# Value products of two attentions as unsplit float32, two query tiles on the two column halves of the array

## The chip, the cores and the metric

One core of a Trainium2 chip runs the whole program in one launch. The metric is the device time in microseconds (us), the median of the runs shown. TensorE (PE) multiplies; VectorE (DVE), ScalarE (ACT) and GpSimd (POOL) do the rest; SyncE (SP) issues most of the loads. Each engine works through its own instructions in order and waits on semaphores for the others.

## The reference, cut to what matters

Two layers run over 512 latent tokens and 256 context tokens, 1024 wide. In each, one projection feeds three head groups, and their outputs are concatenated and projected back. The change touches the last product of two of these groups, probabilities times values:

```
# neighbourhood attention: 8 heads of 64; a query sees 8 x 16 grid neighbours and all 256 context keys
p = softmax(concat([s_loc, s_ctx]))
out = einsum(p[..., :n_keys], v_g) + einsum(p[..., n_keys:], vc)
# differential attention: 4 heads of 64 (two queries and keys of 32); keys are 512 latent + 256 context
p = softmax(s1) - lam * softmax(s2)
out = einsum('bhqk,bkhe->bqhe', p, v)
```

Context tokens attend to the 256 context tokens alone, with the same weights, and only in layer 0, since their result is not needed after it. Everything is float32.

## The kernel before, in words

A large float32 product is made of three passes over split operands: a helper `split` (line 70) writes the value rounded to the short format `F32R` with ACT (line 71, a cast) and the remainder with DVE or POOL (line 75, a subtraction); the three products high x low, high x high and low x high are then summed in PSUM. A product of plain float32 tiles is also possible; the profile shows it as two records of each instruction where an `F32R` product has one.

The stages of a layer, in order: norm and input projection, Fourier groups, differential attention (about 163 to 280 us in layer 0, 1218 to 1330 in layer 1), neighbourhood attention (280 to 452 and 1330 to 1470), output projection, feed-forward. The change lies in the two attention stages.

Both attentions work through steps (head, query tile of 128): tiles 0 to 3 are latent tokens; in layer 0 a fifth step per head handles the 256 context queries. Step n does, in program order:

- `scores` of a later step: the products q k into PSUM, the row maximum (DVE), the exponential (ACT), for differential attention also the mix of two exponentials (DVE, lines 822 to 825);
- `values` of step n-1: the product with the values into bank `do` or `o` (lines 889 and 1154), in a bank, 64 partitions x 512 columns, for the four latent tiles and a bank of its own for the context tile;
- `turn` of step n: PE transposes the probabilities (lines 868, 874 and 1133) into PSUM, and `split` evicts them as high and low part, `dph` or `ph`.

The values of a head are split once per head, by `prep_v` and `values_in`, with ACT and POOL (tiles `dvh`, `vh`). When the last tile of a head is done, ACT copies the bank to `yT` (lines 895, 897, 1093). A latent tile of differential attention has 6 key blocks of 128, so 18 products of 64 x 128; of neighbourhood attention 4 key blocks, so 12. The context tile has 2 key blocks, so 6 products of 64 x 256. The softmax of neighbourhood attention is divided after the values, by `divide` (line 978).

Between steps, `fill` hands PE units of the input projection of later heads (`projection`, line 649, tile `nacc`), so that it has work while DVE and ACT make probabilities. In the second half of neighbourhood attention these are used up, and chunks of the modulation (line 143, tile `m`) stand there, each a product with 32 stationary columns for four column groups of the array. The order on each engine is fixed when the program is built, by a list scheduler that follows dependencies and the priority of program order; pools of two or a few buffers decide what can run ahead.

Of the kernel before, what the change touches and what calls it, by code (L numbers as in the profile page):

```python
# [11 lines left out]
F32 = mybir.dt.float32  # L12
I32 = mybir.dt.int32
F32R = mybir.dt.float32r
# [15 lines left out]
NAH = 8  # L30
# [19 lines left out]
def hybrid_kernel(ctx: ExitStack, tc: tile.TileContext, A, out, dbg=None, stop=None):  # L50
# [409 lines left out]
    for l in range(DEPTH):  # L460
        first, last = l == 0, l == DEPTH - 1
        SL, SR = ("left", "right") if first else ("right", "left")
        nq = 4 if last else 6
# [247 lines left out]

        with ExitStack() as es:
# [62 lines left out]
        with ExitStack() as es:  # L775
            sk = pool(es, f"dstk{l}", 1)
            tq = pool(es, f"dtq{l}", 2)
            wk = pool(es, f"dwk{l}", 1)
            ek = pool(es, f"dek{l}", 2)
            dvp = pool(es, f"dvh{l}", 1)  # L780
# [30 lines left out]

            def prep_v(h):
                vh = dvp.tile([128, 6, 2, 64], F32R, tag="dvh", name="dvh")
                for t0, dv in ((0, dvx), (4, dvc)):
                    n = dv.shape[1]
                    split(vh[:, t0:t0 + n, 0], vh[:, t0:t0 + n, 1], dv[:, :, h * 64:(h + 1) * 64], lo="p")
                return vh
# [41 lines left out]

            def turn(i, e):  # L860
                nonlocal pace
                ph = [wk.tile([128, 768 if i < 4 else 512], F32R, tag=f"dph{z}", name="dph") for z in range(2)]
                ph4 = [p if i < 4 else p.rearrange("p (c i q) -> p c i q", c=2, i=2) for p in ph]
# [12 lines left out]
                return ph  # L876

            def values(h, i, ph):
                nonlocal pace, prev, o, vh
                y = od[h // 2][64 * (h % 2):64 * (h % 2) + 64]  # L880
                if i == 0:
                    vh = prep_v(h)
                    o = po.tile([128, 512], F32, tag="o", name="do")
                    prev = None
                oi, c0, n = (o[0:64, i * 128:i * 128 + 128], 0, 128) if i < 4 else \
                    (po.tile([128, 256], F32, tag="o", name="doc")[0:64], 4, 256)
                jobs = [(vz, pz_, c) for vz, pz_ in ((0, 1), (0, 0), (1, 0)) for c in range(6 - c0)]
                for k, (vz, pz_, c) in enumerate(jobs):
                    pace = pe.matmul(oi, lhsT=vh[:, c0 + c, vz], rhs=ph[pz_][:, c * n:(c + 1) * n],  # L889
                                     start=k == 0, stop=k == len(jobs) - 1)  # L890
                    if k == 0 and i < 4:
                        after(pace, prev)
                prev = pace
                if i == 3:
                    sc.copy(y[:, 0:512], o[0:64])
                elif i == 4:
                    sc.copy(y[:, 512:768], oi)

            pace = prev = o = vh = None
# [25 lines left out]
            values(*steps[-1], ph.pop(n))  # L925
# [72 lines left out]
        with ExitStack() as es:  # L998
# [7 lines left out]
            php = pool(es, f"php{l}", 2)  # L1006
# [42 lines left out]
            def prepare(h):  # L1049
# [5 lines left out]
                H[h] = qT, kT, bia, tq  # L1055
# [29 lines left out]
            def values_in(h):  # L1085
                hs = slice(h % 4 * 64, h % 4 * 64 + 64)
                vh = H[h][3].tile([128, 6, 2, 64], F32R, tag="vh", name="vh")
                split(vh[:, :, 0], vh[:, :, 1], vs[h // 4][:, :, hs], lo="p")
                return vh

            def emit_y(h, o, off, n):
                p0 = 64 * (h % 2)
                sc.copy(yT[h // 2][p0:p0 + 64, off:off + n], o[0:64, 0:n])

            def scores(h, i):
                nonlocal pace
                qT, kT, bia, _ = H[h]
# [31 lines left out]
            def turn(i, sb):  # L1129
# [9 lines left out]
            def values(h, i, ph):  # L1139
                nonlocal pace, prev, o, vh  # L1140
                if i == 0:
                    o = po.tile([128, 512], F32, tag="o", name="o")
                    prev = None
                if i < 4:
                    oi = o[0:64, i * 128:(i + 1) * 128]
                    ks = [(t, c, 1) for c, t in enumerate((i, i + 1, 4, 5) if i < 3 else (4, 5, 0, 3))]
                else:
                    oc = po.tile([128, 256], F32, tag="o", name="oc")
                    oi = oc[0:64].rearrange("p (j q) -> p j q", j=2)
                    ks = [(4, 0, 2), (5, 2, 2)]  # L1150
                n = 0
                for vz, pz_ in ((0, 1), (0, 0), (1, 0)):
                    for t, c, w in ks:
                        pace = pe.matmul(oi, lhsT=vh[:, t, vz], rhs=ph[pz_][:, c:c + w],  # L1154
                                         start=n == 0, stop=n == 3 * len(ks) - 1)
                        if n == 0 and i < 4:
                            after(pace, prev)
                        n += 1
                prev = pace
                if i == 3:  # L1160
                    emit_y(h, o, 0, 512)
                elif i == 4:
                    emit_y(h, oc, 512, 256)
                if i == ni - 1 and h + 1 < NAH:
                    vh = values_in(h + 1)
# [8 lines left out]
            vh = values_in(0)  # L1174
# [6 lines left out]
            for n, (h, i) in enumerate(steps):  # L1181
# [28 lines left out]
                if n:  # L1210
                    values(*steps[n - 1], ph.pop(n - 1))
# [18 lines left out]
            values(*steps[-1], ph.pop(n))  # L1230
# [346 lines left out]
```

## Time and profile before

| | before |
|---|---|
| runs, us | 1916.23, 1918.22, 1919.35 (median 1918.22) |
| profiled execution, us | 1918.2, of which the span from first to last instruction is 1916.4 |
| PE busy | 1807.5 us, 94% of the span |
| DVE, ACT, POOL busy | 1273.3, 788.9, 638.7 us |
| mean granted TensorE clock | 0.983 of full speed |

A row of the grouped view gives line, engine, operation, tile written and tiles read, stationary size and shape, count, then the busy time of the group (overlaps counted once), the mean duration of one, and the idle time of the engine just before, with what ended it. Products are pipelined: their durations overlap, so what one costs in a row of equal ones is the distance between starts, which a timeline shows.

### The profile page before, as it was taken

How to read it: one execution, taken by the hardware profiler on the slowest of the kernel's cores; microseconds unless marked ns; L12 is line 12 of the kernel's file. 1: busy time of each engine (PE TensorE's matmuls, PEld its weight loads, DVE VectorE, ACT ScalarE, POOL GpSimd, SP SyncE). 2: the span in 40 equal slices, each digit the busy share in tenths (PEclk: the TensorE clock that was granted, in tenths of full speed). 3: DMA queues.
4: the chain of work that ended last, by engine and by line, in shares of the span. 5: the costliest groups of instructions: out<-in, count | busy, mean ns of one | idle time of the engine just before them, and what ended most of it. 6: DMA issues, size and time to landing. Idle time of an engine off the chain costs nothing.

```text
span 1916.4 us, 28921 instructions
## 1 busy us (share of the span) xinstructions
PE 1807.5 (94%) x11297; PEld 1528.1 (80%) x11297; DVE 1273.3 (66%) x2494; ACT 788.9 (41%) x1470; POOL 638.7 (33%) x830
## 2 busy tenths in 40 slices
PE   6998989999999999999999989898998999999997
PEld 4787889867877888888888878788987778888885
DVE  4576865566466777767777694686556567777775
ACT  3326755565244222222222252585666243333331
POOL 3465636432141211211111164473833232121122
PEclk9999999999999999999999999999999999999999
DMA  9351021166016322432333013211243233232311
GB/s 284 111 174 45 24 39 32 33 228 194 24 42 204 117 95 97 159 101 73 105 110 110 29 44 112 71 45 36 57 131 122 90 110 110 88 110 88 96 37 44
DMA packets 146720, 183.11 MB, mean 96 GB/s; under 512 B 38200, under 2 KB 108672, under 8 KB 145560
## 3 DMA queue, kind: packets, MB, share of 16 engines
q1 hardware_dynamic: 107056, 157.83, 25.6%
q0 software_dynamic: 5888, 20.26, 3.5%
q10 hardware_dynamic: 33640, 3.19, 1.4%
q8 instruction: 89, 1.46, 0.3%
q14 instruction: 47, 0.39, 0.1%
HBM read 179.07 MB, written 8.07 MB: 98 GB/s over the span
## 4 chain that ended last, share of the span: by engine, by line
PE 79%; DVE 8%; DMA 4%; ACT 3%; issue 2%; POOL 2%; SPq 0%; ACTq 0%; DVEq 0%; POOLq 0%
PE u L1342 25%; PE dps L1406 14%; PE nacc L649 9%; PE uc L1342 6%; PE oacc L1280 6%; PE bank L533 3%; PE o L1154 2%; PE m L143 2%; PE s L1111 1%; DMA w<-w_in 1%; PE tpp L1133 1%; PE do L889 1%; DVE dmx L840 1%; PE u L731 1%; DVE e L825 1%
## 5 line engine op out<-in xcount | busy, mean ns | idle before, releaser
L1342 PE MATMUL u<-hx,uwh 128*128 128x512 f32 (+2 forms) x2160 | 518.5, 393 | 7.8 <-ACT hx L421 2.2
L1342 PEld LDWEIGHTS u<-hx,uwh 128*128 128x128 f32 x2160 | 401.4, 189 | 102.6 <-issue 3.4
L1410 POOL TENSOR_TENSOR res<-res,dm 128x512 f32<-128x512 f32 x110 | 155.8, 1417 | 594.5 <-DVE dm L1409 588.8
L1406 PE MATMUL dps<-wd,gt 128*128 128x512 f32 x1320 | 324.2, 395 | 6.8 <-DVE wd L75 2.8
L1406 PEld LDWEIGHTS dps<-wd,gt 128*128 128x128 f32 x1320 | 248.2, 190 | 64.4 <-DVE dm L1409 4.8
L649 PE MATMUL nacc<-wh,hx 128*128 128x256 f32 x1536 | 212.9, 288 | 4.7 <-ACT wh L71 2.7
L1371 DVE SCALAR_TENSOR_TENSOR ob<-u,cvc,ob 128x504 f32<-128x504 f32 x352 | 153.1, 477 | 93.7 <-ACT ob L1368 92.6
L649 PEld LDWEIGHTS nacc<-wh,hx 128*128 128x128 f32 x1536 | 194.6, 192 | 7.7 <-ACT wh L71 3.1
L1409 DVE TENSOR_TENSOR dm<-dps,g 128x512 f32<-128x512 f32 x220 | 147.9, 684 | 62.0 <-PE dps L1406 58.7
L1368 ACT ACTIVATE ob<-u,cvc 128x512 f32<-128x512 f32 x88 | 68.4, 778 | 200.2 <-PE u L1342 200.2
L1342 PEld LDWEIGHTS uc<-hc,uwh 128*128 128x128 f32 x1056 | 130.3, 190 | 7.5 <-issue 1.7
L1342 PE MATMUL uc<-hc,uwh 128*128 128x256 f32 x1056 | 133.5, 283 | 1.1 <-POOL hc L422 0.5
L75 POOL TENSOR_TENSOR wh<-w,wh 128x512 fp32r<-128x512 f32 x70 | 92.6, 1339 | 56.1 <-ACT wh L71 56.0
L71 ACT CAST uwh<-w 128x1024 fp32r<-128x1024 f32 x88 | 91.2, 1043 | 36.3 <-DMA w<-w_up 23.9
L1280 PE MATMUL oacc<-owh,yh 128*128 128x512 f32 x320 | 101.5, 403 | 1.2 <-DVE y L978 0.8
L75 DVE TENSOR_TENSOR uwh<-w,uwh 128x1024 fp32r<-128x1024 f32 x74 | 96.7, 1313 | 7.4 <-ACT uwh L71 5.8
L71 ACT CAST gt<-g 128x768 fp32r<-128x768 f32 (+1 forms) x44 | 32.1, 729 | 139.1 <-DVE g L1386 139.1
L1410 DVE TENSOR_TENSOR res<-res,dm 128x512 f32<-128x512 f32 x110 | 87.1, 793 | 1.6
L1371 DVE SCALAR_TENSOR_TENSOR ob<-uc,cvc,ob 128x248 f32<-128x248 f32 (+1 forms) x176 | 53.0, 342 | 53.0 <-ACT ob L1367 52.5
L649 PE MATMUL nacc<-wh,hc 128*128 128x256 f32 x624 | 86.4, 289 | 0.3 <-ACT qs L667 0.2
L71 ACT CAST wd<-w 128x1024 fp32r<-128x1024 f32 x44 | 44.8, 1048 | 95.2 <-PE dps L1406 69.5
L75 DVE TENSOR_TENSOR ph<-tpp,ph 128x512 fp32r<-128x512 f32 x72 | 49.3, 688 | 51.3 <-ACT ph L71 51.1
(539 smaller groups left out, 3059.7 us busy)
## 6 DMA issues: line engine op xcount, KB each, us to landing
w<-w_up SPq DMA_DIRECT2D x44, 1024.0 KB, 6.7
w<-w_mod SPq DMA_DIRECT2D x40, 1024.0 KB, 6.1
w<-w_down SPq DMA_DIRECT2D x22, 1024.0 KB, 4.9
w<-w_in SPq DMA_DIRECT2D x18, 1024.0 KB, 5.2
wm<-w_mod SPq DMA_DIRECT2D x8, 1024.0 KB, 9.8
w<-k_dftx POOLq DMA_DIRECT2D x8, 1024.0 KB, 5.3
w<-w_out SPq DMA_DIRECT2D x8, 1024.0 KB, 9.3
bS<-bT POOLq DMA_DIRECT2D x16, 360.0 KB, 8.6
```

The source lines that it names most:

```text
L71: r = sc.copy(dh, src)
L75: (gp if lo == "p" else ve).tensor_tensor(dl, src, dh.bitcast(F32), op=ALU.subtract)
L143: pe.matmul(m[32 * k:32 * k + 32, :], lhsT=cm[:, hf * 4 + k, :], rhs=w[:, k, :], start=hf == 0, stop=hf == 1)
L533: m = pe.matmul(acc[t][:, 0:n], lhsT=kcol(hT[a], k, t), rhs=whs[k][:, b, 0:n], start=k == 0 and z == 0, stop=k == KT - 1 and z == 2)
L649: m = pe.matmul(acc[:, j], lhsT=col(hT[a], k, t + j), rhs=whs[k // 2][:, k % 2, b], start=k == 0 and z == 0, stop=k == KT - 1 and z == 2)
L1280: pe.matmul(accs[t], lhsT=ys[k][a][:, t * 128:(t + 1) * 128], rhs=ow0[k // 2][:, k % 2, b], start=n == 0 and z == 0, stop=n == KT - 1 and ...
L1342: m = pe.matmul(u[2][:, 256 * v:256 * v + 256] if c else cut(u[v]), lhsT=whs[v][:, b, k], rhs=h2[c][a][:, k] if c else cut(h2[c][a][:, k]) ...
L1368: sc.activation(ob[:, 0:512], xu, AF.Identity, bias=b_, scale=w1)
L1371: ve.scalar_tensor_tensor(ob[:, d0:d0 + n], src[:, s0:s0 + n], w_, ob[:, d0:d0 + n], op0=ALU.mult, op1=ALU.add)
L1406: pe.matmul(ps, lhsT=gt[:, ff, a, t * 128:(t + 1) * 128], rhs=wd[ff][:, b, cs_], start=ff == 0 and z == 0, stop=ff == 1 and z == 2)
L1409: ve.tensor_tensor(m, ps, g[:, 0 if key[0] == "x" else 1, cs_], op=ALU.mult)
L1410: (gp if ch == 0 else ve).tensor_tensor(res[key][:, cs_], res[key][:, cs_], m, op=ALU.add)
```

## The change

The value products use the tiles of values as they are, in float32, and the turned probabilities are evicted by one copy instead of a split. `prep_v` and `values_in` are gone. Two query tiles are multiplied together by the new `pair`: tile 0 writes partitions 0 to 63 of the bank and tile 1 partitions 64 to 127, so the first uses stationary columns 0 to 63 of the array and the second 64 to 127; the instructions alternate between the halves. Tiles 2 and 3 make the second pair, the two halves of the context tile the third. Products are made when the second tile of a pair has been turned. The new `emit_pairs` copies the bank to `yT` at the end of a head, one half of the partitions with ACT and the other with DVE. The buffers of the turned probabilities become 3 (differential) and 4 (neighbourhood).

```
+        def pair(o, b, jobs, prev):
+            for n, (v0, v1, r0, r1) in enumerate(jobs):
+                for half, v, r in ((0, v0, r0), (1, v1, r1)):
+                    m = pe.matmul(o[64 * half:64 * half + 64, 128 * b:128 * b + 128], lhsT=v, rhs=r,
+                                  start=n == 0, stop=n == len(jobs) - 1)
+                    if n == 0:
+                        after(m, prev)
+            return m
+
+        def emit_pairs(y, h, o):
+            y3 = y[64 * (h % 2):64 * (h % 2) + 64].rearrange("p (t q) -> p t q", q=128)
+            o3 = o.rearrange("p (b q) -> p b q", q=128)[:, 0:nq // 2]
+            sc.copy(y3[:, 0::2], o3[0:64])
+            ve.tensor_copy(y3[:, 1::2], o3[64:128])
...
-                        split(ph[0][:, c0:c1], ph[1][:, c0:c1], tp)
+                        (ve.tensor_copy if c0 else sc.copy)(ph[:, c0:c1], tp)
...
-                split(ph4[0], ph4[1], tp)
+                ve.tensor_copy(ph, tp.rearrange("p c i q -> p (c i q)"))
...
-            def values(h, i, ph):
+            def values(h, i, p0, p1):
...
-                jobs = [(vz, pz_, c) for vz, pz_ in ((0, 1), (0, 0), (1, 0)) for c in range(6 - c0)]
-                for k, (vz, pz_, c) in enumerate(jobs):
-                    pace = pe.matmul(oi, lhsT=vh[:, c0 + c, vz], rhs=ph[pz_][:, c * n:(c + 1) * n],
-                                     start=k == 0, stop=k == len(jobs) - 1)
...
+                pace = prev = pair(o, i // 2, [(v, v, *r) for v, r in jobs], prev)
+                if i >= (3 if last else 4):
+                    emit_pairs(od[h // 2], h, o)
...
-                if n:
-                    values(*steps[n - 1], ph.pop(n - 1))
+                if n and steps[n - 1][1] not in (0, 2):
+                    values(*steps[n - 1], ph.get(n - 2), ph.get(n - 1))
...
-                ph = [php.tile([128, 4, 128], F32R, tag=f"ph{z}", name="ph") for z in range(2)]
-                turned = split(ph[0], ph[1], tp)
+                ph = php.tile([128, 4, 128], F32, tag="ph", name="ph")
+                turned = (sc.copy if i % 2 else ve.tensor_copy)(ph, tp)
...
+                pace = prev = pair(o, i // 2, jobs, prev)
+                if i == ni - 1:
+                    emit_pairs(yT[h // 2], h, o)
```

What stands where is shown in three places. First PE in layer 0, in the second half of neighbourhood attention, where `o` is the value product, `m` and `gb` belong to the modulation, and `slt` and `rb` to the division. Before:

```order
L1154 MATMUL o<-ph,vh 64x128 x12
L143 MATMUL m<-w,cm 32x512 x4
L189 MATMUL gb<-r,sel 2x512
L963 MATMUL slt<-idf,spf 4x128 x4
L1154 MATMUL o<-ph,vh 64x128 x12
L143 MATMUL m<-w,cm 32x512 x4
L968 MATMUL rb<-slr,hbc 128x512
L1133 MATMUL tpp<-idf,sb 128x128 x4
```

And in the changed program:

```order
L1124 MATMUL tpp<-idf,sb 128x128 x4
L716 MATMUL o<-ph,vs 64x128
L1124 MATMUL tpp<-idf,sb 128x128 x4
L189 MATMUL gb<-r,sel 2x512
L964 MATMUL slt<-idf,spf 4x128 x4
L716 MATMUL o<-ph,vs 64x128 x8
L1102 MATMUL s<-kT,qT 128x256 x4
L143 MATMUL m<-w,cm 32x512 x8
L1102 MATMUL s<-kT,qT 128x256 x4
```

Two runs of 12 products, one for each tile, become one run of 8 for a pair; the row of one product before it is the first of its pair, for the tile turned first, and stands by itself. Counted over the whole program, 1416 value products in 139 unbroken runs become 496 in 107 runs; 39 of the 107 are such a single product.

The second place is PE in the first head of differential attention in layer 0; `ds` are the scores, `dtp` the turned queries of the next head, `do` the value products. Before:

```order
L833 MATMUL ds<-dT 128x512
L833 MATMUL ds<-dT 128x256
L444 MATMUL dtp<-idr,dst 128x128 x3
L443 MATMUL dtp<-xch,dst 128x128
L889 MATMUL do<-dph,dvh 64x128 x4
L846 MATMUL ds<-dT 128x256 x2
L444 MATMUL dtp<-idr,dst 128x128 x2
L889 MATMUL do<-dph,dvh 64x128 x14
```

And in the changed program:

```order
L843 MATMUL ds<-dT 128x512
L843 MATMUL ds<-dT 128x256
L444 MATMUL dtp<-idr,dst 128x128 x3
L443 MATMUL dtp<-xch,dst 128x128
L444 MATMUL dtp<-idr,dst 128x128 x2
L716 MATMUL do<-dph,dvx 64x128 x7
L716 MATMUL do<-dph,dvc 64x128 x4
L649 MATMUL nacc<-wh_1568,hc_184 128x256 x2
```

The 18 products of one tile, in two pieces, become 11 of the 12 of a pair in one piece (the twelfth stands alone further up).

The third place is DVE at the same time, around the eviction of the turned probabilities `dph`; the other rows are row maxima, the mix, and the norm of projected heads. Before:

```order
L669 TENSOR_REDUCE ss<-sq 128x8
L320 TENSOR_SCALAR rx<-ss 128x8
L75 TENSOR_TENSOR dph<-dtpp,dph 128x512
L301 TENSOR_SCALAR rt__1777<-rx 128x8
L75 TENSOR_TENSOR dph<-dtpp,dph 128x256
L840 TENSOR_REDUCE dmx<-ds 128x1
```

And in the changed program:

```order
L669 TENSOR_REDUCE ss<-sq 128x8
L879 COPY dph<-dtpp 128x256
L320 TENSOR_SCALAR rx<-ss 128x8
L301 TENSOR_SCALAR rt__1777<-rx 128x8
L302 TENSOR_SCALAR ry<-rt__1777 128x8
L850 TENSOR_REDUCE dmx<-ds 128x1
```

Two subtractions on DVE are replaced by one copy of the smaller part; the larger part is copied by ACT alone.

## Rows read from the trace of the kernel before

**Rows 1.** The page: busy time, share of the span and instructions.

```profile
PE 1807.5 (94%) x11297; PEld 1528.1 (80%) x11297; DVE 1273.3 (66%) x2494; ACT 788.9 (41%) x1470; POOL 638.7 (33%) x830
```

**Rows 2.** Busy time by stretch: the stretch, its length, PE, PEld, DVE, ACT, POOL.

```profile
163.00:280.00 117.00, 102.92 (x941) 97.20 (x940) 94.30 (x172) 85.86 (x204) 62.04 (x101) 0.97 0.11 26
280.00:452.50 172.50, 163.21 (x1512) 142.56 (x1510) 93.28 (x225) 107.36 (x244) 83.65 (x146) 1.00 0.39 118
1218.00:1330.00 112.00, 100.48 (x925) 95.09 (x925) 80.19 (x138) 79.09 (x169) 57.30 (x101) 0.98 0.06 20
1330.00:1470.00 140.00, 132.40 (x1257) 117.64 (x1255) 80.58 (x188) 88.65 (x183) 71.53 (x129) 0.99 0.37 107
```

**Rows 3.** Groups by line and shape: value products, turned queries and keys, a wide product.

```profile
L1342 PE MATMUL u<-hx,uwh 128*128 128x512 f32 x2064 | 503.0, 396 | 4.9 <-POOL uwh L75 2.0 <-DVE ob L1371 1.9 <-POOL hx L422 0.9
...
L1154 PE MATMUL o<-ph,vh 128*64 128x128 f32 x768 | 58.5, 225 | 2.5 <-DVE ph L75 2.4
L889 PE MATMUL do<-dph,dvh 128*64 128x128 f32 x576 | 48.8, 231 | 11.5 <-DVE dph L75 11.3
...
L439 PE MATMUL dtp<-idr,dst 128*128 128x128 f32 x96 | 12.6, 246 | 2.9 <-DVE dph L75 1.7 <-ACT dT L795 1.0
L444 PE MATMUL dtp<-idr,dst 128*128 128x128 f32 x64 | 9.3, 251 | 9.3 <-DVE dph L75 5.0 <-POOL dst L75 4.3
...
L1154 PE MATMUL oc<-ph,vh 128*64 128x256 f32 x48 | 7.2, 286 | 1.7 <-DVE ph L75 1.7
...
L889 PE MATMUL doc<-dph,dvh 128*64 128x256 f32 x24 | 3.6, 286 | 0.5 <-DVE dph L75 0.5
```

**Rows 4.** Timeline of PE, 344 to 346.2 us: start, length, group, count.

```profile
343.76 1.00 PE L649 MATMUL nacc<-wh,hx 128*128 128x256 f32 x7
344.60 0.88 PE L1154 MATMUL o<-ph,vh 128*64 128x128 f32 x12
345.31 0.93 PE L649 MATMUL nacc<-wh,hx 128*128 128x256 f32 x6
```

**Rows 5.** The chain in order of time, 705 to 720 and 1590 to 1620 us.

```profile
709.76 5.76 PE uc L1342 x48
...
1596.38 19.39 PE u L1342 x84
```

**Rows 6.** Timeline of PE, 514.9 to 516 us, a whole-array float32 product.

```profile
515.16 0.83 PE L386 MATMUL bank<-dg,ones 128*128 128x128 f32 x6
515.83 0.38 PE L394 MATMUL ntp<-idf,res 128*128 128x128 f32 x2
```

**Rows 7.** Timeline of PE, 643 to 647 us, a float32 product on four column groups.

```profile
642.84 1.23 PE L1342 MATMUL uc<-hc,uwh 128*128 128x256 f32 x9
643.99 1.92 PE L143 MATMUL m<-w,cm 128*32 128x512 f32 x16
645.85 1.44 PE L1342 MATMUL u<-hx,uwh 128*128 128x512 f32 x5
```

**Rows 8.** Groups by line and shape, weight loads.

```profile
L1342 PEld LDWEIGHTS uc<-hc,uwh 128*128 128x128 f32 x1056 | 130.3, 190 | 7.5 <-issue 1.7 <-POOL hc L422 1.5 <-ACT hc L421 1.0
...
L1154 PEld LDWEIGHTS o<-ph,vh 128*64 128x64 f32 x768 | 52.3, 135 | 7.8 <-DVE ph L75 5.3 <-issue 1.9
```

**Rows 9.** Groups by line and shape, DVE: subtractions removed, and a copy from PSUM.

```profile
L75 DVE TENSOR_TENSOR ph<-tpp,ph 128x512 fp32r<-128x512 f32 x72 | 49.3, 688 | 51.3 <-ACT ph L71 51.1
...
L75 DVE TENSOR_TENSOR dph<-dtpp,dph 128x512 fp32r<-128x512 f32 x32 | 21.8, 682 | 4.2 <-ACT dph L71 4.1
...
L75 DVE TENSOR_TENSOR dph<-dtpp,dph 128x256 fp32r<-128x256 f32 x32 | 13.2, 412 | 1.0 <-ACT dph L71 1.0
...
L1062 DVE CAST qT<-tp 128x512 fp32r<-128x512 f32 x16 | 11.0, 688 | 14.2 <-PE tp L443 14.0
```

**Rows 10.** Groups by line and shape, ACT: cast of the turned probabilities, and the emission.

```profile
L71 ACT CAST dph<-dtpp 128x512 fp32r<-128x512 f32 x32 | 18.9, 591 | 15.8 <-PE dtpp L868 9.6 <-PE do L889 6.1
...
L1093 ACT COPY y<-o 64x512 f32<-64x512 f32 x16 | 9.2, 576 | 5.8 <-PE o L1154 5.7
```

More of the change, by code (lines that the diff above doesn't have):

```diff
@@ L810, in prep_qk @@
                 qkT[h] = r["q"], r["k"]
[L812 to L817, printed above, removed]
             def mix(e0, e1, sm):
@@ L861, in turn @@
                 nonlocal pace
-                ph = [wk.tile([128, 768 if i < 4 else 512], F32R, tag=f"dph{z}", name="dph") for z in range(2)]
-                ph4 = [p if i < 4 else p.rearrange("p (c i q) -> p c i q", c=2, i=2) for p in ph]
+                ph = php.tile([128, 768 if i < 4 else 512], F32, tag="dph", name="dph")
                 if i < 4:
@@ L874, in turn @@
                         pace = pe.transpose(tp[:, c, i], e[:, i, c * 128:(c + 1) * 128], idf)
[L875 removed]
+                ve.tensor_copy(ph, tp.rearrange("p c i q -> p (c i q)"))
                 return ph
[L878 to L882 removed]
+            def values(h, i, p0, p1):
+                nonlocal pace, prev, o
+                if i == 1:
                     o = po.tile([128, 512], F32, tag="o", name="do")
                     prev = None
[L885 to L899 removed]
+                vh = [(dvx[:, c] if c < 4 else dvc[:, c - 4])[:, h * 64:(h + 1) * 64] for c in range(6)]
+                jobs = [(vh[c], [p[:, c * 128:c * 128 + 128] for p in (p0, p1)]) for c in range(6)] if i < 4 else \
+                    [(vh[4 + c], [p1[:, c * 256 + j * 128:c * 256 + j * 128 + 128] for j in range(2)]) for c in range(2)]
+                pace = prev = pair(o, i // 2, [(v, v, *r) for v, r in jobs], prev)
+                if i >= (3 if last else 4):
+                    emit_pairs(od[h // 2], h, o)
+            pace = prev = o = None
             qkT = {}
@@ L924, in hybrid_kernel @@
                 fill(0, of=rest)
-            values(*steps[-1], ph.pop(n))
+            values(*steps[-1], ph.get(n - 1), ph.get(n))
             fill(0, left[0])
@@ L1083, in prepare @@
                 yield
[L1085 to L1093, printed above, removed]
             def scores(h, i):
                 nonlocal pace
-                qT, kT, bia, _ = H[h]
+                qT, kT, bia = H[h]
                 s = pss.tile([128, 512], F32, tag="s", name="s")
@@ L1142, in values @@
+                return ph
+            def values(h, i, p0, p1):
+                nonlocal pace, prev, o
+                if i == 1:
                     o = po.tile([128, 512], F32, tag="o", name="o")
                     prev = None
+                v = vs[h // 4][:, :, h % 4 * 64:h % 4 * 64 + 64]
                 if i < 4:
-                    oi = o[0:64, i * 128:(i + 1) * 128]
-                    ks = [(t, c, 1) for c, t in enumerate((i, i + 1, 4, 5) if i < 3 else (4, 5, 0, 3))]
-                else:
-                    oc = po.tile([128, 256], F32, tag="o", name="oc")
-                    oi = oc[0:64].rearrange("p (j q) -> p j q", j=2)
-                    ks = [(4, 0, 2), (5, 2, 2)]
@@ L1151, in values @@
[L1151 to L1163, printed above, removed]
@@ L1164, in values @@
-                if i == ni - 1 and h + 1 < NAH:
-                    vh = values_in(h + 1)
+                    ts = [(t, t + 1, 4, 5) if t < 3 else (4, 5, 0, 3) for t in (i - 1, i)]
+                    jobs = [(v[:, t0], v[:, t1], p0[:, c], p1[:, c]) for c, (t0, t1) in enumerate(zip(*ts))]
+                else:
+                    jobs = [(v[:, 4 + c], v[:, 4 + c], p1[:, 2 * c], p1[:, 2 * c + 1]) for c in range(2)]
+                pace = prev = pair(o, i // 2, jobs, prev)
+                if i == ni - 1:
+                    emit_pairs(yT[h // 2], h, o)
@@ L1173, in hybrid_kernel @@
                 fill(1)
-            vh = values_in(0)
             sb, ph = {}, {}
@@ L1209, in hybrid_kernel @@
                 next(prep, None)
-                if n:
-                    values(*steps[n - 1], ph.pop(n - 1))
+                if n and steps[n - 1][1] not in (0, 2):
+                    values(*steps[n - 1], ph.get(n - 2), ph.get(n - 1))
                 fill(1, of=2 * rest)
@@ L1229, in hybrid_kernel @@
                         ow0 = (next(ow, None) if len(ow0) < 2 else None) or ow0
-            values(*steps[-1], ph.pop(n))
+            values(*steps[-1], ph.get(n - 1), ph.get(n))
             for _ in div or ():
```

9 lines of the change are left out of this document (3 added, 6 removed).

## The prediction, on record before the changed kernel ran

> **What bounds the kernel now.** I read the page's totals first. PE is busy for 94% of the span [rows 1], so what the change does to PE's own time comes before all else. Next the busy times of the two attention stages, where alone instructions change: PE stands idle for 14.1 of 117, 9.3 of 172.5, 11.5 of 112 and 7.6 of 140 us, 42.5 us in all [rows 2]. DVE is busy for 94.3 of 117 and 80.2 of 112 us in the two stretches of differential attention and for little more than half of the other two. So a gain has two sources there: shorter products, or less idle time. Third, the groups by line say who ends the idle time: the subtraction that makes the low part of the turned probabilities ends 11.3 + 0.5 us before the products of differential attention, 1.7 + 5.0 us before the turning of its next queries and keys, which need the PSUM bank that the subtraction reads, and 2.4 + 1.7 us before the products of neighbourhood attention: 22.6 of the 42.5 us [rows 3]. The timelines of PE, last, give prices.
>
> **Value products, now.** A run of 12 takes 345.31 - 344.60 = 0.71 us, 0.059 us each; the wide products behind it take 0.93 us where 5 distances of 0.12 and a last duration of 0.28 (the seven ahead: 1.00 = 6 x 0.12 + 0.28) make 0.88, so leaving a run costs 0.05 us [rows 4]. 768 + 576 products at 0.059 are 79.3 us; 48 + 24 products of 256 columns [rows 3] at 0.120, which is what other products of 256 columns take in a long row (5.76 us for 48) [rows 5], are 8.6 us; a wide product follows 77 of the 139 runs, 3.9 us. Sum: 91.8 us.
>
> **Value products, then.** A float32 product leaves two records. On the whole array one with 128 columns takes (515.83 - 515.16) / 6 = 0.112 us [rows 6], so a product is 0.224 us. Do two run side by side on column halves? No row has 64-column halves. The nearest has four groups of 32: 16 records of 512 columns, which at 4 x 0.112 each would be 7.2 us in sequence, go from 643.99 to 645.85, in 1.86 us [rows 7]; four sequences side by side would take 1.79. I take two halves to run fully side by side; in sequence is the other end, below. With half 0 and half 1 alternating, a run of m products lasts as long as its fuller half. Over the 107 runs these add up to 288 products, not 248, because 39 first products stand alone: 288 x 0.224 = 64.5 us.
>
> **Changing between whole array and column groups** has a price. In the same timeline nine products of 256 columns should take 1.08 us and the next group starts after 1.15; the grouped product takes 0.07 us more than 1.79; the five products behind it take 1.44 us where 4 x 0.231 (19.39 us for 84) [rows 5] and a last duration of 0.396 [rows 3] make 1.32. That is 0.07 + 0.07 + 0.12 = 0.26 us in and out [rows 7]. 107 runs x 0.26 = 27.8 us. The bounds are no price at all, since the 64-column products of now come and go without one (start distance of 0.84 us for seven `nacc` ahead of them is 0.12 each) [rows 4], and 0.37, if a load of 64 weight columns, 55 ns by the last rival below, is waited for at both ends. I take 0.26, from the row that has groups. The Trainium skill speaks against the change here: "TensorEngine Tiling (Array Packing)", section "Key Properties", says that changing the tiling mode drains TensorE. By that rule the 128 x 64 products of now should pay as well, and [rows 4] show 0.05 at most; where groups are really used [rows 7] the trace agrees with it.
>
> PE's own time is thus 64.5 + 27.8 = 92.3 against 91.8: +0.5 us. The side-by-side gain is spent on the changes.
>
> **Evictions.** In differential attention a turned tile now passes ACT's cast of 512 columns (0.59 us) [rows 10], then DVE's subtractions of 512 and 256 (0.68 + 0.41) [rows 9]: 1.68 us from the last transposition to the first product. Then ACT copies 512 columns while DVE copies 256: 0.59, shorter by 65%. In neighbourhood attention a cast and a subtraction of 0.69 become one copy, at DVE's 0.69 for 512 columns from PSUM [rows 9]: 1.28 to 0.69, 46%. In proportion, the waits shrink by 0.65 x 18.5 + 0.46 x 4.1 = 13.9 us. The bounds are 0 and 22.6. Behind such a wait the next one stands: DVE's maximum and mix remain, in a stretch where DVE was busy for four fifths [rows 2]; I take a fifth off: 11.1 us.
>
> DVE's own load falls from 49.3 + 21.8 + 13.2 us of subtractions [rows 9] to about 40 x 0.69 + 32 x 0.41 = 41, plus the emission below; ACT loses the casts of half of the neighbourhood tiles and all casts of values, POOL the subtractions of values. I count nothing for these beyond the waits: neither ACT nor POOL reaches three quarters of a stretch [rows 2], and PE hides them. If PE had no units left to fill with, as in the last 60 us of each attention stage, up to the remaining idle time would answer too; that is inside the 22.6.
>
> **The added wait.** Each head's bank is now emptied by DVE as well, 24 copies of 64 x 384 or 256, between 0.41 and 0.69 us [rows 9]; ACT's copies of this kind took 0.58 and waited 5.8 us in all for the products, over 16 [rows 10]. Queued behind DVE's are the row maxima and the mix or bias of the next tiles; ACT's exponentials wait for those, and PE's transposes after them. If DVE waits as ACT did, 24 x 0.36 = 9 us of DVE are lost, less than the 43 us that it gains. I put it at 0, with 4 us as the other end. A product alone at the head of a pair needs one turned tile only, and no queue of loads is passed by anything.
>
> **The sum**, against the profiled execution of 1918.2 us, which equals the median of the runs to 0.02: 1918.2 + 0.5 - 11.1 = 1907.6, say 1908.
>
> **Rivals.**
> *No change-over price* for halves of 64, as [rows 4] have it for that width: 27.8 us less, 1880. For it: that width is in the trace without a price. Against: those products are of the one-pass kind and use one half only, and the float32 ones on groups pay.
> *The waits stay.* Something else stands right behind the subtraction, the exponential or the mix, and PE meets it: 1918.7, and up to 1923 if DVE's emission costs its 4 us. For it: the stretch where DVE is busiest also has the most idle time of PE [rows 2]. Against: over half of that time ends with the subtraction itself.
> *In sequence.* The halves share a bank and an order, and each product waits for the one ahead: 496 x 0.224 = 111.1 instead of 64.5, so +46.6 us, 1954. This decides from the first run on. Against: [rows 7], a factor of four for four groups in the same bank.
> *Loads in the open.* The weights of a half are loaded only when its products have ended. A load of 64 columns less costs 190 - 135 = 55 ns less [rows 8], so 576 records in sequence grow by 0.055: 31.7 us more, 1939, slower. Against: in [rows 7] 16 records, each with its load, took 0.07 us more than the products alone. The Trainium skill, "TensorE: Matmul & The Clock Gate", section "The mechanism", allows a load beside running products only where row groups differ, and column halves share theirs; by that rule this rival would hold, and [rows 7] do not bear it out.
>
> **How the numbers follow.** My case gets 0.56, with its own range of 1895 to 1921 from the bounds of the waits; no price 0.14; waits stay 0.16; in sequence 0.07; loads in the open 0.07. A difference under 0.2%, 3.8 us, is about what a measurement of this kernel can't tell from none. My case is faster by more with 0.45 and within it with 0.11; with 0.14 from the second, faster is 0.59. Within: 0.11 + 0.10 = 0.21. Slower: 0.06 + 0.07 + 0.07 = 0.20. The range runs from 1877 to 1927: both cases beyond 1927 stay out, and the lower half of the fast one, 0.2 together.
>
> **What would show it.** A run of 8 value products (16 records) of about 0.9 us between its first start and the last, with starts of the two halves a few ns apart: side by side; 1.8 us: in sequence. Starts of the next whole-array product about 0.1 us later than the distance in a row: the change-over. Idle time of PE in the four stretches of about 30 us, and of it hardly any ended by evictions on DVE: the waits. The prediction is wrong if PE's time in these stretches moves by over 10 us either way, or if the idle time stays above 38 us.

## The result, and the profile after

The changed kernel takes 1897.9 us, the median of 4 runs (1892.87 to 1900.08), against 1918.78 (1916.23 to 1920.87) for the kernel before on the same chip: a ratio of 0.9888, 95% interval 0.9864 to 0.9912. The forecast was 1908 with a range of 1877 to 1927. The sign and the mechanism held; the gain of 20.9 us is twice the 10.6 of the sum. The profiled execution took 1896.75 us, 1895.0 of it span.

The page of the changed kernel, busy times, to be read against [rows 1]:

```profile
PE 1797.4 (95%) x10873; PEld 1497.0 (79%) x10873; DVE 1245.9 (66%) x2454; ACT 738.6 (39%) x1350; POOL 613.6 (32%) x798
```

The span is 21.4 us shorter and PE only 10.1 us less busy. To see where, I cut both traces at the first product of each stage. The columns are those of [rows 2]; in order come differential and neighbourhood attention of layer 0, then of layer 1. Before:

```profile
161.40:283.61 122.21, 108.13 (x985) 102.33 (x984) 96.37 (x175) 88.61 (x209) 65.39 (x105) 0.97 0.13 32
283.61:452.79 169.18, 159.59 (x1480) 138.95 (x1479) 92.46 (x223) 105.85 (x241) 81.94 (x144) 1.00 0.38 115
1230.86:1334.74 103.88, 93.65 (x878) 88.78 (x877) 77.91 (x131) 75.34 (x161) 56.99 (x93) 0.98 0.11 33
1334.74:1468.49 133.75, 126.42 (x1216) 112.53 (x1214) 79.41 (x186) 85.10 (x177) 67.18 (x125) 1.00 0.35 102
sum 529.02, PE 487.79 PEld 442.59 DVE 346.14 ACT 354.90 POOL 271.50; mean PE 121.95 PEld 110.65 DVE 86.54 ACT 88.72 POOL 67.88
```

After:

```profile
161.45:277.56 116.11, 106.60 (x897) 95.26 (x895) 88.53 (x163) 78.24 (x178) 59.14 (x98) 0.97 0.13 31
277.56:445.48 167.92, 159.90 (x1368) 130.76 (x1367) 86.70 (x217) 89.46 (x204) 76.29 (x137) 0.99 0.37 115
1224.39:1327.29 102.90, 94.41 (x781) 85.70 (x781) 74.35 (x122) 67.47 (x137) 54.43 (x85) 0.94 0.15 37
1327.29:1453.96 126.67, 124.55 (x1088) 104.56 (x1087) 69.90 (x170) 71.17 (x151) 60.98 (x118) 1.00 0.35 105
sum 513.60, PE 485.46 PEld 416.28 DVE 319.49 ACT 306.34 POOL 250.83; mean PE 121.37 PEld 104.07 DVE 79.87 ACT 76.58 POOL 62.71
```

The four stages lose 15.4 us: PE's own time 2.3, its idle time (length less busy) 13.1, from 41.2 to 28.1. The stretch between the layers takes 0.8 us more (778.1 and 778.9). From the first product of layer 1's output projection to the end it is 447.9 before (1916.4 - 1468.49) and 441.0 after (1895.0 - 1453.96): 6.9 us in which PE makes the same products, only the first of them in another order. PE stands idle there for 19.2 us before and 18.8 after, so nearly all of the 6.9 us is products that take longer.

The groups by line and shape that answer to [rows 3, 9, 10]:

```profile
L716 PE MATMUL o<-ph,vs 128*64 128x128 f32 x576 | 51.1, 284 | 0.5 <-ACT ph L1127 0.5
...
L716 PEld LDWEIGHTS o<-ph,vs 128*64 128x64 f32 x576 | 35.3, 137 | 12.7 <-issue 5.4 <-PE s L1102 0.9 <-ACT kst L71 0.8
...
L878 PE MATMUL dtpp<-idf,e 128*128 128x128 f32 x192 | 29.6, 285 | 11.5 <-DVE e L835 8.9 <-ACT dT L812 1.1 <-DVE rt__12172 L301 0.8
...
L1127 DVE COPY ph<-tpp 128x512 f32<-128x512 f32 x40 | 27.3, 687 | 25.1 <-PE tpp L1124 24.7
...
L879 ACT COPY dph<-dtpp 128x512 f32<-128x512 f32 x32 | 18.9, 591 | 20.2 <-PE dtpp L878 20.0
...
L879 DVE COPY dph<-dtpp 128x256 f32<-128x256 f32 x32 | 13.3, 415 | 4.7 <-PE dtpp L878 4.6
...
L716 PE MATMUL do<-dph,dvx 128*64 128x128 f32 x128 | 12.2, 282 | 0.9 <-ACT dph L879 0.9
```

PE's waits for evictions on DVE, 22.6 us before, are nearly gone. In their place stands a wait of 8.9 us of the turning for the mix (L835).

The timeline of PE around a run of value products in the changed kernel (answers to [rows 4]):

```profile
327.69 0.29 PE L439 MATMUL tp<-idr,kst 128*128 128x128 f32 x2
327.91 1.09 PE L716 MATMUL o<-ph,vs 128*64 128x128 f32 x14
328.93 0.98 PE L649 MATMUL nacc<-wh,hc 128*128 128x256 f32 x6
...
1449.77 1.09 PE L716 MATMUL o<-ph,vs 128*64 128x128 f32 x16
1450.79 0.60 PE L964 MATMUL slt<-idf,spf 128*4 128x128 f32 x4
```

Eight products, 16 records, take 1.02 us from their first start to the next group's. In sequence, at the 0.112 us of a record [rows 6], they would need 1.79: the halves run side by side. The `nacc` group behind needs 0.98 where 0.88 would do, reckoned as in [rows 4]: there is a change-over. The row of 14 records takes 1.02 us too. Its pair has eight products, of which the first stands alone further up, so one half still has four. The row of 16 holds the seven that are left of such a pair and the first of the next; the run of eight in the first place shown under "The change", with a single product before it, must be put together in the same way and isn't one pair.

### The profile page after: what moved, and what is told of

It reads as the page before. It is cut to its first block, busy times and chain, and to the rows that moved or that the text cites. A ratio compares the mean times of both kernels' runs of the same rounds, so it can differ in the third digit from the quotient of the medians.

```text
span 1895.0 us, 27868 instructions
## 1 busy us (share of the span) xinstructions
PE 1797.4 (95%) x10873; PEld 1497.0 (79%) x10873; DVE 1245.9 (66%) x2454; ACT 738.6 (39%) x1350; POOL 613.6 (32%) x798
## 4 chain that ended last, share of the span: by engine, by line
PE 84%; DVE 6%; DMA 4%; ACT 2%; issue 2%; POOL 2%; SPq 0%; ACTq 0%; DVEq 0%; POOLq 0%
PE u L1319 25%; PE dps L1383 14%; PE nacc L649 12%; PE uc L1319 7%; PE oacc L1257 6%; PE bank L533 3%; DMA w<-w_in 3%; PE o L716 2%; PE m L143 2%; PE s L1102 2%; PE tpp L1124 2%; PE do L716 1%; PE ds L843 1%; PE dtpp L878 1%; PE u L748 1%
## 5 line engine op out<-in xcount | busy, mean ns | idle before, releaser
L649 PEld LDWEIGHTS nacc<-wh,hx 128*128 128x128 f32 x1536 | 195.5, 193 | 10.2 <-ACT wh L71 4.2
L75 DVE TENSOR_TENSOR uwh<-w,uwh 128x1024 fp32r<-128x1024 f32 x74 | 97.3, 1322 | 10.8 <-ACT uwh L71 9.3
L649 PEld LDWEIGHTS nacc<-wh,hc 128*128 128x128 f32 x624 | 80.0, 196 | 2.7 <-issue 1.9
```

Of the source, the lines that this page charges most:

```text
L75: (gp if lo == "p" else ve).tensor_tensor(dl, src, dh.bitcast(F32), op=ALU.subtract)
L649: m = pe.matmul(acc[:, j], lhsT=col(hT[a], k, t + j), rhs=whs[k // 2][:, k % 2, b], start=k == 0 and z == 0, stop=k == KT - 1 and z == 2)
```

## The experiments

Each was compared with the kernel before on the same chip. The first four shared a chip, the next four a second and three more a third; the last had its own. On all of them the kernel before took 1917.4 to 1919.0 us. Stage lengths are cut as above, each from one profiled execution.

**The changed kernel again**, unedited.

> The changed kernel once more, for a second profile and more times. Theory (waits): about 1898 us, and again some 28 us of idle time of TensorE in the two attention stages where the kernel before has 41. The first profile is also 7 us shorter from the first product of the second layer's output projection to the end, where no instruction was changed: if that is the clock, the stretch is longer here (441 to 448 us) in step with the stretches at half rate; if the change does it in some other way, it is 441 again.

1897.76 us (1894.83 to 1902.14), ratio 0.9901 (0.9881 to 0.992). Its stages sum to 511.8 us with 28.3 idle, and its stretch behind them takes 440.9: the accounting above is no chance of one execution.

**The eviction in two steps again**: each goes through ACT and then DVE, the products stay as changed.

```
+        def two_step(ph, tp):
+            r = sc.copy(ph, tp)
+            ve.tensor_tensor(ph, tp, ph, op=ALU.max)
+            return r
...
-                turned = (sc.copy if i % 2 else ve.tensor_copy)(ph, tp)
+                turned = two_step(ph, tp)
```

> The changed kernel, but the turned probabilities are evicted in two steps as before: ScalarE copies, then VectorE rewrites them from PSUM and that copy (the larger of two equal numbers). Products as in the changed kernel. Theory (waits: PE's own time is even, the shorter eviction is the gain): most of the gain goes, 8 to 14 us longer, 1906 to 1912, with idle time before products back to 37 us or more. Rival (products: the paired products are the gain): 0 to 3 us longer, 1898 to 1901. The rival that the load taken off the other engines is the gain expects the same as the theory here and is told apart by another run.

1912.67 us, ratio 0.9982 (0.9969 to 0.9995): 14.9 above the changed kernel. Its waits of PE in differential attention of layer 0 (columns: waited for, us in total, times, longest):

```profile
PE do L716 <- DVE dph L724: 9.3, 5, 3.6
```

The old wait is back, with new products. PE's time in the four stages is 488.7, 3.2 above the changed kernel, and its idle time 37.9, 9.8 above. So the short eviction, with the load it takes off DVE, is three quarters of the gain; this run doesn't tell the two apart. Two of its stages, the differential one of layer 0 and the neighbourhood one of layer 1:

```profile
164.89:291.60 126.71, 110.77 (x897) 97.20 (x895) 98.81 (x179) 85.05 (x198) 57.55 (x97) 0.96 0.13 32
...
1340.09:1469.56 129.47, 126.02 (x1088) 105.20 (x1086) 78.69 (x186) 78.88 (x167) 60.87 (x118) 1.00 0.34 102
```

What is left, 5 us against the kernel before, lies elsewhere. The two differential stages take 228.8 us (226.1 before, 219.0 in the changed kernel), so there the new products by themselves bring nothing. The two neighbourhood stages take 297.8 (302.9 before, 294.6 in the changed kernel), and the stretch behind them takes 440.8: there most of the gain stays without the short eviction.

**One half of the array after the other**: all products of half 0, then all of half 1.

```
-            for n, (v0, v1, r0, r1) in enumerate(jobs):
-                for half, v, r in ((0, v0, r0), (1, v1, r1)):
+            for half in range(2):
+                for n, job in enumerate(jobs):
...
+                prev = m
```

> The changed kernel with all products of one half of a pair before those of the other half, in the same two column halves. 496 products then come one after another where 288 places did, in 112 runs where there were 107. Theory (side by side is worth its full price on the path): 208 x 0.218 + 5 x 0.28 = 47 us longer, 1945. Rival (PE has slack in these stages, so its own time hardly counts): under 15 us longer.

1913.34 us, ratio 0.9976 (0.9963 to 0.999): 15.6 above the changed kernel, far from the theory's 47 and just outside the rival. One run in the timeline, then the sum over the four stages (columns as above):

```profile
1466.31 1.97 PE L716 MATMUL o<-ph,vs 128*64 128x128 f32 x16
1468.20 0.60 PE L965 MATMUL slt<-idf,spf 128*4 128x128 f32 x4
```

```profile
sum 530.53, PE 517.13 PEld 447.90 DVE 316.48 ACT 308.96 POOL 250.43; mean PE 129.28 PEld 111.98 DVE 79.12 ACT 77.24 POOL 62.61
```

Sixteen records now take 1.89 us in place of 1.02, so running side by side is real. Of the 31.7 us of added PE time only 16.9 lengthen the stages; the other 14.7 fill idle time, which falls from 28.1 to 13.4.

**No product alone**: the half that needs the later tile goes first and the other is ordered behind it.

```
-                for half, v, r in ((0, v0, r0), (1, v1, r1)):
+                for half, v, r in ((1, v1, r1), (0, v0, r0)):
...
                     if n == 0:
                         after(m, prev)
+                        prev = m
```

> The changed kernel, but the half whose tile is turned last goes first in a pair and the other half is ordered behind it, so that no first product stands alone: 73 runs of value products instead of 107, 252 places instead of 288. Theory (every change between whole array and halves costs 0.28 us on the path, every place 0.218): 34 x 0.28 + 36 x 0.218 = 17 us shorter, 1881. Rival (the changes are hidden by waits, or later products wait longer): 0 to 5 us shorter, 1893 to 1898.

1894.24 us, ratio 0.9885 (0.9866 to 0.9905): 3.5 below the changed kernel, inside the spread of both. The sum over the four stages:

```profile
sum 512.41, PE 476.87 PEld 412.75 DVE 317.94 ACT 307.32 POOL 249.97; mean PE 119.22 PEld 103.19 DVE 79.49 ACT 76.83 POOL 62.49
```

PE is busy for 8.6 us less, with 73 runs for 107, and idle for 7.4 us more. (The profiled execution, 1900.1 us, was the slowest of the five, so these sums lie rather too high.) PE waits for probabilities, so a shorter product pays for little of its length: the rival, as the experiment before shows from the other side.

**The kernel before again**, unedited.

> The kernel before, unchanged, for a second profile. In the first pair of profiles the four attention stages account for 15.3 of the 21 us between the two kernels, and 6.9 us lie behind them, from the first product of the output projection of layer 1 to the end (447.9 us before, 441.0 after), where no instruction differs. Theory A, the tail belongs to the kernel: before comes to its output projection with PE idle and at half the granted clock, and this profile shows 446 to 449 again. Theory B, it is chance of one execution: 440 to 443, and the sum of the four stages carries the whole difference. The four attention stages: 527 to 531 us by either theory.

1918.29 us (1915.51 to 1920.02). Its stages sum to 528.7, the stretch behind them to 446.5: theory A.

**The splits of the values put back**, into tiles that nothing reads.

```
+                    vh = wk.tile([128, 6, 64], F32R, tag="vh", name="vh")
+                    split(vh, vh, vs[h // 4][:, :, h % 4 * 64:h % 4 * 64 + 64], lo="p")
```

> The changed kernel with the splits of the values put back on ACT and POOL, once per head, into tiles that nothing reads. Theory A, the gain is the shorter eviction: a head's split is hidden behind PE, so the time is that of the changed kernel to 3 us more (1898 to 1901). Theory B, part of the gain is the load taken off ACT and POOL (50 and 25 us less busy than before): 5 us more or above (1903 to 1908).

1892.73 us, ratio 0.9879 (0.986 to 0.9899): 5 us less than the changed kernel and below both expectations, though the intervals of the two ratios overlap. Work was added and the time did not rise, so the load on ACT and POOL costs nothing that shows, as forecast. What fell most is differential attention of layer 1, 97.3 us for 102.9. This is DVE in the changed kernel at the end of that stage, and the turning that waits:

```profile
1312.40 0.69 DVE L1034 COPY res<-brwe 64x128 f32<-64x128 f32 x1 [1.73 <-DMA brwe<-bS]
...
1313.12 1.22 DVE L1036 COPY res<-brwe 64x128 f32<-64x128 f32 x1
1314.38 0.17 DVE L832 RECIPROCAL drr<-dsum 128x1 f32<-128x1 f32 x1
...
1314.58 0.91 DVE L834 SCALAR_TENSOR_TENSOR dcf<-dsum,lam,drr 128x1 f32<-128x1 f32 x1
...
1315.52 1.02 DVE L835 SCALAR_TENSOR_TENSOR e<-e,dcf 128x768 f32<-128x768 f32 x1
1316.69 1.51 PE L878 MATMUL dtpp<-idf,e 128*128 128x128 f32 x6 [4.70 <-DVE e L835]
```

Two copies of the next stage's bias stand ahead of the last mix on DVE and wait for a load; PE waits 4.70 us behind them. They are slow here as well, 0.69 and 1.22 us where the shortest take 0.25 to 0.27, with POOL at work beside them; no run tests whether that is why. With the value splits back, the mix came ahead of both:

```profile
1307.55 0.22 DVE L835 SCALAR_TENSOR_TENSOR dcf<-dsum,lam,drr 128x1 f32<-128x1 f32 x1
1307.81 1.02 DVE L836 SCALAR_TENSOR_TENSOR e<-e,dcf 128x768 f32<-128x768 f32 x1
...
1310.52 0.82 DVE L1038 COPY res<-brwe 64x128 f32<-64x128 f32 x1 [0.24 <-DMA brwe<-bS]
```

**Each attention alone.** First the change in differential attention only (the neighbourhood stage keeps lines such as the first below), then the reverse (the differential stage keeps the second).

```
-                turned = (sc.copy if i % 2 else ve.tensor_copy)(ph, tp)
+                turned = split(ph[0], ph[1], tp)
...
-                        (ve.tensor_copy if c0 else sc.copy)(ph[:, c0:c1], tp)
+                        split(ph[0][:, c0:c1], ph[1][:, c0:c1], tp)
```

> The change made in differential attention alone; neighbourhood attention as before. Theory A, waits: 18.5 of the 22.6 us of idle time that the subtractions ended were in differential attention, so most of the gain comes here: 1918 - 10 to -14, 1904 to 1908. Theory B, by the stage lengths of the two profiles (differential attention 226.0 to 219.1, neighbourhood attention 303.0 to 294.6, behind both 447.9 to 441.0): 7 us from this part, 1911, and the rest from the other.

1904.18 us, ratio 0.9934 (0.9916 to 0.9953): 13.2 below the kernel before, as theory A had it. The two differential stages take 117.7 and 97.3 us.

> The change made in neighbourhood attention alone; differential attention as before. Theory A, waits: only 4.1 us of the idle time that the subtractions ended were here, so 1914 to 1918. Theory B, by the stage lengths: 8 us from the stage itself, 1910, and 7 more if the stretch behind it belongs to this part, 1903.

1905.03 us, ratio 0.9943 (0.9925 to 0.9961): 12.4 below, far more than theory A's 0 to 4. The neighbourhood stages take 167.7 and 126.4 us, the stretch behind them 441.0; in the kernel changed in differential attention alone that stretch is 443.5. The two gains add up to 25.6 us and together gave 20. In neither half-changed kernel did the differential stage of layer 1 meet the bias copies above (97.3 us, and 103.8 with the old eviction), so they are the likely loss; the next run tests it.

**The bias copies on POOL**, in the changed kernel; in the next two it is kept.

```
-                ve.tensor_copy(be[0:64, 0:128].rearrange("p (c r) -> p c r", r=8),
+                gp.tensor_copy(be[0:64, 0:128].rearrange("p (c r) -> p c r", r=8),
```

> The changed kernel with the two copies that place a head's bias (the tiles written from brwe, in the neighbourhood stage) on POOL instead of DVE. Theory A: in differential attention of layer 1 (102.9 us) PE stands 4.7 us before the last turning because on DVE these two copies, waiting 1.7 us for their load, stand ahead of the last mix; with them gone from DVE the stage takes 97 to 98 us, as in the kernels whose order had them behind it (97.3), and the time is 1892 to 1894. Theory B: the wait only moves to the score or the eviction behind it, or POOL is late with the next splits: 1896 to 1900.

1889.93 us (1884.52 to 1891.72), ratio 0.9848 (0.9826 to 0.987). The differential stages:

```profile
160.60:273.21 112.61, 105.67 (x892) 94.65 (x890) 85.09 (x158) 77.97 (x177) 60.27 (x102) 0.97 0.12 27
...
1217.63:1315.36 97.73, 92.10 (x782) 83.64 (x781) 69.82 (x119) 68.67 (x139) 56.82 (x93) 0.98 0.16 39
```

Layer 1 does what theory A said. Layer 0 gains 3.5 us as well; there a wait of 2.4 us of `dtpc` for the mix's factor `dcf` is gone. The four stages sum to 505.7 us, 7.9 below the changed kernel (in the profiled execution of 1884.5 us, the fastest of the four), and the time falls below theory A's 1892.

**Bias on POOL, and no product alone.**

> The kernel with the bias on POOL, and besides the half that needs the later tile first and the other half behind it, so that no product stands alone (73 runs of value products instead of 107, 252 places instead of 288). Theory A: PE's shorter work in the attention stages, 8.6 us, is turned into idle time again for the most part, since the probabilities come no faster: 2 to 4 us below the kernel with the bias on POOL. Theory B: with that wait on DVE gone PE sets the stages, and the full 8 us show.

1887.4 us (1886.51 to 1887.81), ratio 0.9839 (0.9821 to 0.9857): 2.5 below the kernel just above, within theory A, though the intervals overlap. PE's time in the four stages falls by 10.5 us to 471.9, and its idle time rises by 9.8 to 33.1. This is the lowest time of the study. With the bias on POOL both kernels beat the changed kernel as it was run again (0.9881 to 0.992, an interval above both); which of the two is faster stays open.

**Bias on POOL, and ACT evicts all of `dph`.**

```
-                        (ve.tensor_copy if c0 else sc.copy)(ph[:, c0:c1], tp)
+                        sc.copy(ph[:, c0:c1], tp)
```

> The kernel with the bias on POOL, and the smaller part of the turned probabilities of differential attention (128 x 256, 0.42 us on DVE) evicted by ACT as well, behind the larger one. Theory A, the delay of the eviction is what PE meets: it grows from 0.59 to about 0.97 us, so 2 to 6 us slower than the kernel with the bias on POOL. Theory B, the load of DVE is what PE meets (it loses 32 x 0.42 = 13 us): 2 to 6 us faster.

1890.15 us, ratio 0.9855 (0.9834 to 0.9876): 0.2 from its base, so neither theory. The longer delay and the lighter DVE may cancel, or neither is met; this is inconclusive, and it leaves open which of the two the gain of the short eviction comes from.

**The kernel before with the bias copies on POOL.**

> The kernel before with the two bias copies of a head on POOL instead of DVE, and nothing else. Moving them gave the changed kernel about 8 us. Theory A, the wait that they made belongs to the change: with shorter evictions the bias copies came to stand ahead of the last mix of a layer; in the kernel before the subtractions decide, and moving the copies gives 0 to 3 us (1915 to 1918). Theory B, the copies cost both kernels alike: 6 us or more (below 1912), and the 8 us have nothing to do with the change.

1915.4 us, ratio 0.998 (0.9971 to 0.9989): 2.6 below the kernel before, within theory A. The differential stages:

```profile
162.72:280.72 118.00, 107.82 (x980) 102.11 (x979) 93.20 (x170) 87.98 (x207) 65.77 (x106) 0.97 0.12 28
...
1229.13:1333.09 103.96, 93.75 (x879) 88.86 (x878) 77.93 (x131) 75.25 (x161) 57.00 (x93) 0.98 0.11 34
```

Layer 1 stays as it was (103.9), so the 5.2 us that the changed kernel got back there are the change's own: its new order put the copies in PE's way. Layer 0 is another matter. Its differential stage falls from 122.2 to 118.0 us, as the changed kernel's fell (its neighbourhood stage gives 1.8 back). So the kernel before met the copies there too. In its timeline one waits 1.59 us for its load ahead of a subtraction, and PE waits behind both:

```profile
270.08 0.26 DVE L1033 COPY bi<-brwe 64x128 f32<-64x128 f32 x1 [1.59 <-DMA brwe<-bS]
...
272.32 0.68 DVE L75 TENSOR_TENSOR dph<-dtpp,dph 128x512 fp32r<-128x512 f32 x1
...
273.05 0.69 PE L889 MATMUL do<-dph,dvh 128*64 128x128 f32 x4 [4.15 <-DVE dph L75]
```

With the copies on POOL this wait is 2.13 us. And with them on POOL on both sides, the change is worth 25.5 us (1915.4 to 1889.9, measured on two chips).

## Why the forecast held, and where its size failed

By the signs that the forecast named it held: PE's time in the stages moved by less than 10 us, and the idle time came well under 38.

**PE's own time: held.** The forecast was +0.5 us; in the stages it fell by 2.3. Both of its parts are there in kind. A run of eight has four places on each half, 0.22 us each. The change-over was sized at 0.26 us and is a little larger. Of the 1.02 us, 8 x 0.109, the distance of records in the trace, is 0.87; the other 0.15 is change-over. To that come about 0.10 ahead (the run starts 0.22 us after the start of two `tp` products that stand about 0.06 apart) and 0.10 behind (`nacc`): 0.34 for this run. Over all runs of the trace the medians are 0.09 ahead and 0.06 behind, so 0.30 is typical. Counted from the first start of each run to the next product, idle time left out, value products took 96.7 us in 139 runs and now take 80.3 in 107. With 107 x 0.15 to 0.20 for what lies outside the runs, and 77 x 0.05 before, that is 96 to 102 us now against 101. The sum had 92.3 against 91.8: both sides too low, the difference right. The side-by-side gain is spent on the changes, as forecast.

The Trainium skill, "TensorEngine Tiling (Array Packing)", section "Key Properties", says that a change of tiling mode drains the array; the 0.30 to 0.34 us agree. The Trainium skill, "TensorE: Matmul & The Clock Gate", section "The mechanism", says that loads overlap running products only where row groups differ, by which the rival of loads in the open would hold. The trace does not bear it out: record pairs follow each other every 0.109 us though their loads take 0.137 each.

**The waits: right in kind, wrongly placed.** The forecast was -11.1 us, measured -13.1, and the two-step eviction gives 14.9 back. But the agreement is luck: two errors of opposite sign. In differential attention the forecast was 0.65 x 18.5 less a fifth, 9.6 us, and idle time there fell by 6.3 (14.1 to 9.5 and 10.2 to 8.5). "Behind such a wait the next one stands" was right, its fifth too small: the bias copies, which I never looked at, gave layer 1 a wait of 4.7 us (3.5 in the second profile) that the kernel before did not have. And in layer 0 a part of the wait that I put down to the subtraction was theirs: with the copies on POOL in the kernel before, the products `do` wait for it 7.8 us, not 11.3. In neighbourhood attention the forecast was 1.5 us, and idle time fell by 6.8 (9.6 to 8.0 and 7.3 to 2.1). I counted only waits that ended with the subtraction there; for the lighter engines I wrote "I count nothing for these beyond the waits". PE's waits in layer 1's neighbourhood stage, before:

```profile
PE rb L968 <- ACT slr L966: 3.4, 2, 2.4
PE s L1111 <- DVE nm L1116: 2.5, 3, 1.0
PE o L1154 <- DVE ph L75: 1.1, 4, 0.3
```

After, the first is the only one left:

```profile
PE rb L969 <- ACT slr L967: 1.5, 3, 0.7
```

Of these, the wait for the score's DVE work (`nm`) and most of the wait for the division (`slr`) ended elsewhere than at the subtraction, and went all the same. The shorter eviction is not the main reason: with the eviction in two steps the neighbourhood stages have 12.4 us of idle time, against 16.9 before and 10.1 in the changed kernel. So two thirds of the fall came with the new products and their order. In differential attention the whole fall goes with the eviction: 25.5 us idle in two steps, against 24.3 before and 18.0.

**The edge of the stage: not in the sum.** I let the change end with the stages "where alone instructions change". Before, ACT made seven casts `yh` of the next stage ahead of the division's small cast `slr`, PE waited 2.45 us, and began the projection:

```profile
1463.50 3.74 ACT L71 CAST yh<-y 128x512 fp32r<-128x512 f32 x7
...
1467.15 0.57 ACT L966 CAST slr<-slt 4x512 fp32r<-4x512 f32 x1
...
1467.77 0.79 PE L968 MATMUL rb<-slr,hbc 4*128 4x512 f32 x1 [2.45 <-ACT slr L966]
```

After, `slr` stands ahead of them:

```profile
1452.31 0.57 ACT L967 CAST slr<-slt 4x512 fp32r<-4x512 f32 x1
...
1452.93 0.49 PE L969 MATMUL rb<-slr,hbc 4*128 4x512 f32 x1 [0.52 <-ACT slr L967]
1453.29 3.75 ACT L71 CAST yh<-y 128x512 fp32r<-128x512 f32 x7
```

The first 11 us of the projection before (the columns are those of the stages; the granted clock is third from the end):

```profile
1468.49:1479.49 11.00, 10.15 (x34) 7.61 (x34) 5.69 (x5) 4.88 (x7) 6.73 (x6) 0.72 0.33 104
```

With the change in neighbourhood attention alone:

```profile
1460.58:1471.58 11.00, 10.22 (x43) 7.95 (x44) 11.00 (x13) 7.51 (x11) 3.93 (x5) 1.00 0.27 99
```

After PE stood for 2.45 us, the granted clock averages 0.72, part of the stretch at the lower level of 1.2 GHz, and 34 products fit in; after the short wait 43 do. Nine products at 0.23 us are 2.1 us. The four profiles with the neighbourhood stage as before have 0.61 to 0.72 there, the ten with it changed have 1.00. This part of the 6.9 us belongs to the change. The rest are further stretches at a lower clock, about 90 and 426 us into the projection: the first profile of before has both, the second the first of them, the changed kernel neither. The clock accounts for the whole difference: read in windows of 1 us from here to the end, PE's busy time times the share of the clock that it lacked comes to 10.3 and 8.6 us in the two profiles of before, and to 3.1 and 3.0 in those of the changed kernel. But the kernel with the value splits put back, whose neighbourhood products are as changed, has both later stretches and took 444.9 us. That the change removes them is not shown.

**The rivals.** No change-over price: refuted, about 0.3 us a run are there. The waits stay: refuted for the subtraction; yet its mechanism (the mix right behind) was real, and PE waited 8.9 us for it. In sequence: refuted by the run of 1.02 us, and its price was too high as well: the kernel that runs one half after the other lost 15.6 us, not 46.6, because idle time took up nearly half of what PE really grew by, 31.7. Loads in the open: refuted by the same run.

**The added wait on DVE** for the emission was left at 0. DVE stood idle before the bank's copies for 17.1 us (2.3 + 6.9 + 2.6 + 5.3, the four groups of L726) where the forecast had 9; what that cost PE, and what the larger number of buffers gave, no run here measured by itself.

## What to carry to other kernels

Where PE is 94% busy yet waits again and again for its next operand, the eviction between two products can be worth more than the products themselves: making it one step, with the load that this took off DVE, gave some 15 us, while 8.6 us less of PE's time gave 3.5. When an eviction gets shorter, look in the order of its engine for what a scheduler may now put ahead of the next urgent instruction, above all a copy that waits for a load. A wait that the profile puts down to one instruction may belong to what stands ahead of it on the same engine. And follow a change over the edge of its stage: a wait there was paid here a second time, in the granted clock of the next stage.

## What the hardware showed that I had not expected

- Entering and leaving the column halves with float32 products costs about 0.3 us a run (0.34 in the run shown), while before one-pass products of 64 columns in the same place cost 0.05 [rows 4].
- Two column halves of 64 run side by side, loads included: 16 records in 1.02 us against 1.89 in turn, of which the change-over is 0.15 either way.
- In four profiles an idle stretch of about 2.45 us in PE is followed by 11 us at a mean granted clock of 0.61 to 0.72; in ten others, with no wait above 0.8 us there, by 1.00.
